# A two-block transformer kernel: expert selection issued in step with the weight splits, masks as full-row matmuls, and a rebuilt head

## The chip, the cores and the metric

The kernel runs on one core of one Trainium2 chip, in one launch. The metric is the device time of that core in microseconds (us), the median of three runs. One further execution was recorded by the hardware profiler, and every line of a view below comes from it.

## What is computed

256 tokens of width 1024 pass through two transformer blocks, everything in float32:

```
h = modulate(rms_norm(x), shift, scale)            # shift, scale, gate from silu(c) @ ada_w
z = h @ w_in + b_in                                # first block: q, k, v, gates, attention q, k, v
hm = mlstm_chunkwise(conv-silu(q, k), v, gates)    # 4 heads of 128
qa, ka = rope(aq, positions), rope(ak, positions)  # 8 heads of 64
ya = causal softmax attention(qa, ka, va)
x += g1 * ((sig(ga)*(ym @ p_mlstm) + sig(gb)*(ya @ p_moba)) @ w_out)
x += g2 * ((silu(h2 @ w_gate) * (h2 @ w_up)) @ w_down)
# second block
x += gate_m * (concat(pool_mixer, ssd_mixer) @ w_out_2)   # state-space mixer, 16 heads
q = h @ w_query; s1, s2 = q1 @ sub_keys1, q2 @ sub_keys2  # 8 heads, 128 keys each
v1, i1 = top_k(s1, 16); v2, i2 = top_k(s2, 16)
top_s, pos = top_k(v1[:, None] + v2[None, :], 16)         # 16 of 256 sums
out = sum over the chosen experts of softmax(top_s) * gelu(h . expert_down[i]) * expert_up[i]
x += gate_f * out; return rms_norm(x)
```

The kernel doesn't gather experts: it forms h . expert_down for all 16384 of them (128 slabs of 128x1024, the function `dblock`), multiplies by a sparse weight that the selection gives (`gstage`), and multiplies with all of expert_up.

## The kernel before

**Weights and matmuls.** Every weight slab is a 128x1024 float32 tile (512 KB) that comes by DMA on SyncE's queue. The slab is split into a high part `hi` (ScalarE, L213) and a low part `lo = raw - hi` (L218 on VectorE, or L216 on GpSimd), and every product is three fp32r matmuls, hi by high, hi by low, lo by high (`mm3`, L273). A block of 128 output rows takes 24 such matmuls of 256 columns. `prep` (L198) runs the list `items` two slabs ahead of the matmuls; `hi` and `lo` have three buffers each, raw slabs four and two more (`raw`, `ada`). `cur["gp"]` says that every gp-th split goes to GpSimd; 0 means none.

**Order.** The program is written in the order of the functions. A scheduler with a timing model of its own then fixes the order of instructions on each engine. `after(ins, prev)` (L89) is an edge without a semaphore that keeps `ins` behind `prev` on one engine. Background work is written as generators in `gens`; `tick()` (L295) emits one step of the first one, once per block or so.

**Head** (L128 to L455). The row c is loaded and spread over 128 partitions by two one-row matmuls (L380); the V bias row `bv` is loaded (4 KB, L138) and spread likewise (L423, L424). The squares of x are summed: four tiles of 128x512, squared on ScalarE (two) and GpSimd (two, L412), added on VectorE (L415), then summed over partitions by two matmuls (L316) in float32. `rstd` follows (Ln, Exp on ScalarE), then for each of eight k steps: two columns of the modulation (L230, VectorE), the modulated tile of x (L332 to L334), two slabs split, 36 matmuls of 256 columns (L452 to L454) and 6 of 512 (`mv`). At the end of the k steps `late1` (L393) loads constants, among them the positions (`posr`, spread by DMA) and the constants' tiles `cst0`, `cst1`.

**Rope angles** (L489 to L510). Behind the k steps the angles are reduced into plus or minus pi by nine VectorE instructions on 128x256, then Sin, Abs, Sin on ScalarE give `sin_t` and `cos_t`, which `rope` (L631) reads.

**Attention scores** (`moba`, L659). For the two halves of the tokens (tt = 1, then 0) and four groups c, one PSUM tile `ps` holds two heads: each a float32 matmul with 64 rows (L671; two instructions each) on partitions 0 to 63 or 64 to 127, and a mask added by a bf16 matmul of 128 rows and 128 columns (L672). VectorE takes row maxima (L674, L675), ScalarE the exponentials (L679), VectorE normalizes (L690), and TensorE transposes (L699 to L701). A score PSUM tile is one of five `sp` tiles.

**State-space masks** (L922 to L933). For 16 heads: a matmul of 48 rows and 384 columns (L929), two bf16 mask matmuls of 128 columns (L930, L931), two exponentials on ScalarE (L932, L933).

**Expert selection** (`topk`, L1083). Four generators, one per half of the heads and half of the tokens, 16 to 18 steps each: searches of eight maxima in 128 or 256 values (MAX8, FIND_INDEX8, MATCH_REPLACE8), the table of sums `cand`, one-hot comparisons `eq`, the softmax `gat`. A step is emitted after each of the query blocks 8 to 15 and of the first 64 slabs of expert_down; gp is 2 for the query blocks from 8 on and for slabs 0 to 27, then 0.

**Sparse weights** (`gstage`, L1194). 32 groups of eight tokens per half: one-hot tiles A and B on VectorE (L1198 to L1205), 16 small matmuls (L1210), a product into W (L1214). Half 0 runs beside slabs 64 to 127 of expert_down, half 1 beside expert_up.

## Time and profile before

| | us |
|---|---|
| median of three runs | 1427.33 (1427.19 to 1429.57) |
| the profiled execution | 1433.29 |
| its span, first to last instruction | 1431.5 |
| TensorE matmul busy | 1389.7 (97%) |
| VectorE busy | 1155.1 (81%) |
| ScalarE busy | 708.8 (50%) |
| GpSimd busy | 61.3 (4%) |

Matmuls overlap: one of 256 columns is shown as 0.28 us long, and the next one begins 0.12 us after it. So a busy TensorE may still lose time, and the number of matmuls that begin in a stretch says more than its busy share. The granted clock is 0.989 of full speed over the span, so it fell somewhere.

### The profile page before, as it was taken

Reading aid. Unit: us, or ns where it says so; the run is one execution under the profiler, and the core shown is the slowest. Engines: PE = TensorE matmul, PEld = TensorE weight load, DVE = VectorE, ACT = ScalarE, POOL = GpSimd, SP = SyncE. Lnnn points to the kernel's source line nnn. Section 1 sums busy time; section 2 is a strip of 40 time slices with the busy share of each in tenths; the row PEclk is TensorE's granted clock in tenths of the full one; section 3 lists DMA queues with packets and bytes.
Section 4 is the critical chain, followed back from the end, with each engine's and each line's share of the span. In section 5 each row is a group of like instructions: output and inputs, shape, how many; then the busy total and the mean of one; then the engine's idle time right before and its main releaser. Section 6 shows DMA issues by size and latency. Waiting matters only on the chain.

```text
span 1431.5 us, 28913 instructions
## 1 busy us (share of the span) xinstructions
PE 1389.7 (97%) x11842; PEld 1341.2 (94%) x11842; DVE 1155.1 (81%) x1995; ACT 708.8 (50%) x1052; POOL 61.3 (4%) x50
## 2 busy tenths in 40 slices
PE   8999989999999999998899999999999999999997
PEld 6888779899999788998899999999999999999997
DVE  7999558988888597789956978989689999675554
ACT  4555465554546846555554544444444443444443
POOL 0000000000000000123420000000000000000001
PEclk9999889999999999999999999999999999999999
DMA  9988416699995353554455555555655555676663
GB/s 319 341 289 314 148 47 192 229 350 343 330 317 207 104 155 125 163 161 149 162 188 181 177 166 174 163 165 172 180 164 161 177 161 172 200 215 213 208 205 103
DMA packets 78921, 285.92 MB, mean 200 GB/s; under 512 B 8786, under 2 KB 9186, under 8 KB 78660
## 3 DMA queue, kind: packets, MB, share of 16 engines
q1 hardware_dynamic: 78484, 282.60, 60.6%
q8 instruction: 93, 1.52, 0.4%
q0 software_dynamic: 304, 1.47, 0.3%
q14 instruction: 40, 0.33, 0.1%
HBM read 282.99 MB, written 1.05 MB: 198 GB/s over the span
## 4 chain that ended last, share of the span: by engine, by line
PE 85%; DVE 10%; ACT 2%; DMA 2%; issue 1%; SPq 0%; DVEq 0%; ACTq 0%
PE pp L274 17%; PE pp L276 17%; PE pp L275 17%; PE sp L1271 9%; PE sp L1274 8%; PE sp L1275 8%; DVE lo L218 3%; PE pp L1210 2%; ACT hi L213 1%; PE sp L671 1%; DMA raw<-in_wst 0%; DVE raw L230 0%; DMA ada<-in_wst 0%; DVE M L965 0%; PE sp L929 0%
## 5 line engine op out<-in xcount | busy, mean ns | idle before, releaser
L213 ACT ACTIVATE hi<-raw 128x1024 fp32r<-128x1024 f32 x382 | 404.6, 1060 | 562.7 <-PE pp L275 282.9
L218 DVE TENSOR_TENSOR lo<-raw,hi 128x1024 fp32r<-128x1024 f32 x364 | 450.3, 1238 | 141.3 <-ACT hi L213 140.5
L276 PE MATMUL pp<-nH,lo 128*128 128x256 f32 x1064 | 301.6, 285 | 16.1 <-DVE lo L218 16.1
L274 PE MATMUL pp<-nH,hi 128*128 128x256 f32 x1064 | 300.0, 283 | 1.5 <-ACT fs L107 0.9
L275 PE MATMUL pp<-nL,hi 128*128 128x256 f32 x1064 | 300.3, 283 | 0.0
L1271 PE MATMUL sp<-wHL,hi 128*128 128x256 f32 x992 | 279.5, 283 | 0.0
L1274 PE MATMUL sp<-wHL,hi 128*128 128x256 f32 x992 | 277.7, 281 | 0.0
L1275 PE MATMUL sp<-wHL,lo 128*128 128x256 f32 x992 | 273.8, 281 | 0.0
L274 PE MATMUL pp<-hH,hi 128*128 128x256 f32 (+1 forms) x824 | 237.0, 288 | 1.3 <-ACT sg L721 1.3
L276 PE MATMUL pp<-hH,lo 128*128 128x256 f32 (+1 forms) x824 | 234.6, 285 | 0.0
L275 PE MATMUL pp<-hL,hi 128*128 128x256 f32 (+1 forms) x824 | 233.6, 284 | 0.0
L276 PEld LDWEIGHTS pp<-nH,lo 128*128 128x128 f32 x1064 | 200.2, 189 | 19.4 <-DVE lo L218 19.3
L274 PEld LDWEIGHTS pp<-nH,hi 128*128 128x128 f32 x1064 | 200.7, 189 | 2.1 <-ACT fs L107 1.1
L275 PEld LDWEIGHTS pp<-nL,hi 128*128 128x128 f32 x1064 | 200.5, 189 | 0.1
L1271 PEld LDWEIGHTS sp<-wHL,hi 128*128 128x128 f32 x992 | 188.2, 190 | 0.0
L1274 PEld LDWEIGHTS sp<-wHL,hi 128*128 128x128 f32 x992 | 188.0, 189 | 0.0
L1275 PEld LDWEIGHTS sp<-wHL,lo 128*128 128x128 f32 x992 | 185.9, 190 | 0.0
L274 PEld LDWEIGHTS pp<-hH,hi 128*128 128x128 f32 x824 | 157.1, 191 | 2.7 <-ACT sg L721 1.5
L276 PEld LDWEIGHTS pp<-hH,lo 128*128 128x128 f32 x824 | 157.2, 191 | 1.1 <-issue 0.7
L275 PEld LDWEIGHTS pp<-hL,hi 128*128 128x128 f32 x824 | 157.3, 191 | 0.7 <-issue 0.5
L1214 DVE SCALAR_TENSOR_TENSOR W<-pp,W 128x512 f32<-128x512 f32 x64 | 86.1, 1346 | 22.3 <-PE pp L1210 22.3
L213 ACT ACTIVATE hi<-ada 128x1024 fp32r<-128x1024 f32 x52 | 55.1, 1059 | 67.3 <-PE pp L275 37.9
(442 smaller groups left out, 2146.9 us busy)
## 6 DMA issues: line engine op xcount, KB each, us to landing
raw<-in_edn SPq DMA_DIRECT2D x128, 512.0 KB, 3.6
raw<-in_eup SPq DMA_DIRECT2D x128, 512.0 KB, 4.2
raw<-in_ada SPq DMA_DIRECT2D x64, 512.0 KB, 5.0
raw<-in_win SPq DMA_DIRECT2D x34, 512.0 KB, 4.4
ada<-in_ada SPq DMA_DIRECT2D x32, 512.0 KB, 5.1
raw<-in_wgu SPq DMA_DIRECT2D x32, 512.0 KB, 4.5
ada<-in_win SPq DMA_DIRECT2D x18, 512.0 KB, 4.5
raw<-in_wdn SPq DMA_DIRECT2D x15, 512.0 KB, 5.8
```

The costliest lines, as they stand in the source:

```text
L213: S.activation(hi, raw, AF.Copy)
L218: cur["lo"] = V.tensor_tensor(lo, raw, hi.bitcast(F32), OP.subtract)
L274: m = PE.matmul(ps, lh, rh, start=start, stop=False)
L275: PE.matmul(ps, lh, rl, start=False, stop=False)
L276: PE.matmul(ps, ll, rh, start=False, stop=stop)
L671: PE.matmul(ps[:, j * T:j * T + ns], ro[rows, r, tt * P:(tt + 1) * P], ro[rows, 4 + r, :ns], start=True, stop=False)
L1210: PE.matmul(ps[:, t * 64:(t + 1) * 64], A[:, t].rearrange("p n d -> p (n d)"), B[:, j, t].rearrange("p n d -> p (n d)"), start=(j == 0), s ...
L1214: V.scalar_tensor_tensor(wv, ps.rearrange("p (t n) -> p t n", t=GT), 1.0 / GSC, wv, OP.mult, OP.mult)
L1271: m = PE.matmul(o, hi[:, b], wH, start=first, stop=False, skip_group_check=True)
L1274: PE.matmul(o, hi[:, b], wL, start=False, stop=False, skip_group_check=True)
L1275: return PE.matmul(o, lo[:, b], wH, start=False, stop=last, skip_group_check=True)
```

## The change

Six edits. (1) The bias row `bv` comes by a DMA that spreads it over 128 partitions (512 KB, in `late1`), in place of a 4 KB load and two matmuls. (2) Squares 1 and 3 of x move from GpSimd to VectorE, and the two halves are added before a single summing matmul. (3) The rope angles are computed in the head; `posr` and a small tile `inv` (inverse frequencies and pi/2) are loaded from GpSimd's queue. (4) Scores: two groups share a step, their 64-row matmuls alternate between the two halves of the partitions, and one fp32r mask matmul of 256 columns serves both heads of a PSUM tile. (5) State-space masks: the operand is padded with zeros to 128 rows, and the two mask matmuls become one of 256 columns in fp32r; the mask operands are made on ScalarE. (6) Expert selection: edges put the steps of `topk` and the first instruction of each `gstage` group behind the newest `lo` on VectorE; gp becomes 4, from query block 8 to slab 55.

```diff
+    posr = q1.tile([P, T], I32, name="posr")
+    G.dma_start(posr, bass.AP(tensor=I["pos"].tensor, offset=I["pos"].offset, ap=[[0, P], [1, T]]))
+    inv = const.tile([P, 2], F32, name="inv")
+    G.dma_start(inv, I["inv"])
-    dma(brow[0:1], I["bv"])
...
+    def paced(ins):
+        after(ins, cur["lo"])
+        return ins
...
         def late1():
             dma(cst[0], I["cst0"])
-            dma(posr, bass.AP(tensor=pa.tensor, offset=pa.offset, ap=[[0, P], [1, T]]))
+            load_bias_row(bv, I["bv"])
             dma(wif, I["wif"])
             dma(cst[1], I["cst1"])
...
+        trig = q1.tile([P, 4, T], F32, name="trig", tag="qk")
+        ang = trig[:, 0]
+        V.tensor_copy(ang, posr)
+        V.tensor_scalar(ang, ang, inv[:, 0:1], None, op0=OP.mult)
...
         sx = q1.tile([P, 512], F32, name="sx", tag="rt")
...
-                    G.tensor_tensor(sq, src, src, OP.mult)
+                    V.tensor_tensor(sq, src, src, OP.mult)
...
-        for k in range(2):
-            sumsq_mm(nps[:, :T], sx[:, k * T:(k + 1) * T], k, 2)
+        V.tensor_tensor(sx[:, :T], sx[:, :T], sx[:, T:], OP.add)
+        sumsq_mm(nps[:, :T], sx[:, :T], 0, 1)
-        for j in range(2):
-            bps = sp()
-            PE.matmul(bps, ones[0:1], brow[0:1, j * 512:(j + 1) * 512], start=True, stop=True)
-            S.activation(bv[:, j * 512:(j + 1) * 512], bps, AF.Copy)
...
-                    ps = sp()
-                    rows = slice(64 * (c % 2), 64 * (c % 2) + 64)
-                    for j in range(2):
-                        r = 2 * (c // 2) + j
-                        PE.matmul(ps[:, j * T:j * T + ns], ro[rows, r, tt * P:(tt + 1) * P], ro[rows, 4 + r, :ns], start=True, stop=False)
-                        PE.matmul(ps[:, j * T + tt * P:j * T + ns], identb, trib, start=False, stop=True)
+                    if c % 2 == 0:
+                        pair = [sp(), sp()]
+                        for j in range(2):
+                            r = 2 * (c // 2) + j
+                            for i, ps in enumerate(pair):
+                                rows = slice(64 * i, 64 * i + 64)
+                                PE.matmul(ps[:, j * T:j * T + ns], ro[rows, r, tt * P:(tt + 1) * P], ro[rows, 4 + r, :ns],
+                                          start=j == 0, stop=False, skip_group_check=True)
+                        for ps in pair:
+                            PE.matmul(ps.rearrange("p (g s) -> p g s", g=2)[:, :, tt * P:ns], identr,
+                                      trir[:, None, :].to_broadcast([P, 2, P]), start=False, stop=True, skip_group_check=True)
+                    ps = pair[c % 2]
...
-        ArS = q3.tile([48, 384], F32R, name="ArS")
+        ArS = q3.tile([P, 384], F32R, name="ArS")
+        G.memset(ArS.bitcast(F32), 0.0)
...
-                PE.matmul(ab[:, :P], identb, trib, start=False, stop=False, skip_group_check=True)
-                PE.matmul(ab[:, T:384], identb, trib, start=False, stop=True, skip_group_check=True)
+                PE.matmul(ab.rearrange("p (g s) -> p g s", g=2)[:, :, :P], identr, trir[:, None, :].to_broadcast([P, 2, P]),
+                          start=False, stop=True, skip_group_check=True)
...
-                    V.max(v[:, h, 0:8], s_[:, h])
+                    paced(V.max(v[:, h, 0:8], s_[:, h]))
...
-                cur["gp"] = 2
+                cur["gp"] = 4
...
-            cur["gp"] = 2 if n2 < 28 else 0
+            cur["gp"] = 4 if n2 < 56 else 0
...
-            V.tensor_tensor(A, iob.rearrange("p (n d) -> p n d", d=2)[:, None].to_broadcast([P, GT, 64, 2]),
+            paced(V.tensor_tensor(A, iob.rearrange("p (n d) -> p n d", d=2)[:, None].to_broadcast([P, GT, 64, 2]),
```

## Rows read from the trace of the kernel before

**Rows 1.** Busy time by stretch: us, then busy (instructions) per engine, clock, DMA, GB/s
```profile
16.00:60.00 44.00, 43.24 (x297) 39.41 (x297) 41.41 (x75) 18.90 (x24) 0.00 (x0) 1.00 0.97 339
...
167.00:184.00 17.00, 17.00 (x65) 13.15 (x65) 6.86 (x24) 8.71 (x30) 0.00 (x0) 0.50 0.10 32
...
473.40:493.70 20.30, 20.30 (x139) 15.42 (x138) 11.30 (x20) 17.43 (x44) 0.00 (x0) 1.00 0.39 118
...
608.00:728.00 120.00, 107.64 (x889) 105.62 (x888) 114.88 (x360) 62.27 (x92) 44.36 (x17) 1.00 0.48 155
728.00:775.00 47.00, 47.00 (x399) 47.00 (x398) 18.39 (x15) 21.30 (x32) 2.40 (x1) 1.00 0.64 202
...
1040.00:1215.00 175.00, 175.00 (x1838) 173.63 (x1838) 170.80 (x229) 71.91 (x69) 0.00 (x0) 1.00 0.53 165
```

**Rows 2.** Waits, 608 to 728 us: total us, times, longest
```profile
PE pp L276 <- DVE lo L218: 11.9, 8, 2.4
```

**Rows 3.** Timeline in expert selection, GpSimd and VectorE: start, duration, instruction
```profile
678.37 2.39 POOL L216 TENSOR_TENSOR lo<-raw,hi 128x1024 fp32r<-128x1024 f32 x1 [2.64 <-ACT hi L213]
...
678.58 3.26 DVE L218 TENSOR_TENSOR lo<-raw,hi 128x1024 fp32r<-128x1024 f32 x1
```

**Rows 4.** VectorE by line, 608 to 728 us: busy us, mean ns, idle before
```profile
L218 DVE TENSOR_TENSOR lo<-raw,hi 128x1024 fp32r<-128x1024 f32 x21 | 31.9, 1522 | 4.8 <-ACT hi L213 4.8
...
L1097 DVE MAX8 v<-s 128x8 f32<-128x128 f32 x24 | 5.1, 273 | 2.8 <-ACT s L1093 2.8
```

**Rows 5.** Timeline of TensorE through the attention scores
```profile
161.76 0.70 PE L671 MATMUL sp<-ro 64*128 64x256 f32 x2
162.39 0.23 PE L672 MATMUL sp<-trib,identb 128*128 128x128 bf16 x1
162.55 0.70 PE L671 MATMUL sp<-ro 64*128 64x256 f32 x2
...
176.76 0.79 PE L671 MATMUL sp<-ro 64*128 64x128 f32 x2
...
177.71 0.79 PE L671 MATMUL sp<-ro 64*128 64x128 f32 x2
...
186.05 0.28 PE L699 MATMUL sp<-cst,P 128*128 128x128 f32 x1
```

**Rows 6.** Timeline of TensorE: three column tiles of 32, six instructions
```profile
134.45 0.65 PE L585 MATMUL sp<-E,ones 128*32 128x256 f32 x6
134.91 0.41 PE L586 MATMUL sp<-E,ones 128*32 128x128 f32 x6
```

**Rows 7.** Waits, 161.7 to 190 us
```profile
ACT P L107 <- DVE nm L675: 7.1, 3, 4.8
```

**Rows 8.** Timeline of TensorE in the state-space masks, two heads
```profile
473.47 0.44 PE L929 MATMUL sp<-ArS,id 48*128 48x384 f32 x1
...
474.06 0.44 PE L929 MATMUL sp<-ArS,id 48*128 48x384 f32 x1
```

**Rows 9.** Waits, 38 to 120 us
```profile
PE pp L274 <- ACT sg L721: 1.3, 1, 1.3
```

**Rows 10.** The rope angles' tile: four of the nine, ns min/median/max, first and last start
```profile
L505 DVE SCALAR_TENSOR_TENSOR trig<-trig x4: 417/418/426, 61.3 to 64.9; 128x256 f32<-128x256 f32 x4
```

**Rows 11.** Timeline of the head, TensorE and ScalarE
```profile
12.28 3.78 PE L423 MATMUL sp<-vm,ones 1*128 1x512 f32 x4
...
14.16 0.49 ACT L333 ACTIVATE hH<-mt,mod 128x256 fp32r<-128x256 f32 x1
...
15.98 1.22 PE L452 MATMUL sp<-hH,hi 128*128 128x256 f32 x4
```

**Rows 12.** Timeline in the sparse weights, VectorE and TensorE
```profile
1108.83 0.77 DVE L1205 TENSOR_TENSOR B<-B,gd 128x512 f16<-128x512 f16 x2
1109.50 1.23 DVE L218 TENSOR_TENSOR lo<-raw,hi 128x1024 fp32r<-128x1024 f32 x1
...
1110.72 0.64 PE L1210 MATMUL pp<-B,A 128*128 128x64 f16 x16
```

More of the change, by code (lines that the diff above doesn't have):

```diff
@@ L43 @@
 NPRM = _o
-CST = [("ident", 128), ("iota", 128), ("invf", 1), ("half_pi", 1)]
+CST = [("ident", 128), ("iota", 128)]
 CS1 = [("mA", 256), ("tri", 128), ("selr", 512), ("sel4", 512), ("selt", 128), ("rotT", 128)]
@@ L388, in two_block_kernel @@
         cst[1] = q1.tile([P, NCST[1]], F32, name="cst1")
-        posr = q1.tile([P, T], I32, name="posr")
         bv = q1.tile([P, D], F32, name="bv")
@@ L403, in two_block_kernel @@
         cos_t = q1.tile([P, T], F32, name="cos_t")
+        trig = q1.tile([P, 4, T], F32, name="trig", tag="qk")
+        ang = trig[:, 0]
+        V.tensor_copy(ang, posr)
+        V.tensor_scalar(ang, ang, inv[:, 0:1], None, op0=OP.mult)
+        kk = trig[:, 1]
+        V.tensor_scalar(kk, ang, 1.0 / TWO_PI, MAGIC, op0=OP.mult, op1=OP.add)
+        k2 = trig[:, 2]
+        V.tensor_scalar(k2, kk, MAGIC, None, op0=OP.subtract)
+        rest = TWO_PI
+        parts = []
+        for bits in (5, 13, 21):
+            c = np.floor(rest * 2.0 ** bits) / 2.0 ** bits
+            parts.append(float(c))
+            rest -= c
+        parts.append(float(rest))
+        for c in parts:
+            V.scalar_tensor_tensor(ang, k2, -c, ang, OP.mult, OP.add)
+        V.tensor_scalar(ang, ang, PI_F, -PI_F, op0=OP.min, op1=OP.max)
+        act(sin_t, ang, AF.Sin)
+        aab = trig[:, 3]
+        S.activation(aab, ang, AF.Abs)
+        act(cos_t, aab, AF.Sin, scale=-1.0, bias=inv[:, 1:2])
         sx = q1.tile([P, 512], F32, name="sx", tag="rt")
@@ L488, in two_block_kernel @@
         silu_set()
-        trig = q1.tile([P, 4, T], F32, name="trig", tag="ro")
-        ang = trig[:, 0]
-        V.tensor_copy(ang, posr)
-        V.tensor_scalar(ang, ang, cs_("invf"), None, op0=OP.mult)
-        kk = trig[:, 1]
-        V.tensor_scalar(kk, ang, 1.0 / TWO_PI, MAGIC, op0=OP.mult, op1=OP.add)
-        k2 = trig[:, 2]
-        V.tensor_scalar(k2, kk, MAGIC, None, op0=OP.subtract)
-        rest = TWO_PI
-        parts = []
-        for bits in (5, 13, 21):
-            c = np.floor(rest * 2.0 ** bits) / 2.0 ** bits
-            parts.append(float(c))
-            rest -= c
-        parts.append(float(rest))
-        for c in parts:
-            V.scalar_tensor_tensor(ang, k2, -c, ang, OP.mult, OP.add)
-        V.tensor_scalar(ang, ang, PI_F, -PI_F, op0=OP.min, op1=OP.max)
-        act(sin_t, ang, AF.Sin)
-        aab = trig[:, 3]
-        S.activation(aab, ang, AF.Abs)
-        act(cos_t, aab, AF.Sin, scale=-1.0, bias=cs_("half_pi"))
         zp = [q1.tile([P, 3 + T], F32, name="zp%d" % i) for i in range(4)]
@@ L653, in two_block_kernel @@
         yaH, yaL = ya[:, 0], ya[:, 1]
-        identb = q1.tile([P, P], BF, name="identb")
-        V.tensor_copy(identb, ident)
-        trib = q1.tile([P, P], BF, name="trib")
-        V.tensor_copy(trib, cs_("tri"))
+        identr = q1.tile([P, P], F32R, name="identr")
+        S.activation(identr, ident, AF.Copy)
+        trir = q1.tile([P, P], F32R, name="trir")
+        S.activation(trir, cs_("tri"), AF.Copy)
         def moba():
@@ L881, in two_block_kernel @@
         cbT = q3.tile([P, 2, 384], F32, name="cbT")
[L882 to L883 removed]
+        ArS = q3.tile([P, 384], F32R, name="ArS")
+        id16 = q3.tile([P, 16], F32R, name="id16")
+        G.memset(ArS.bitcast(F32), 0.0)
+        G.memset(id16.bitcast(F32), 0.0)
         S.activation(id16[0:32], ident[0:32, 0:16], AF.Copy)
         S.activation(id16[32:48], ident[0:16, 0:16], AF.Copy)
[L886 to L889 removed]
+        identr = q3.tile([P, P], F32R, name="identr")
+        S.activation(identr, ident, AF.Copy)
+        trir = q3.tile([P, P], F32R, name="trir")
+        S.activation(trir, cs_("mB"), AF.Copy)
         yv = q3.tile([P, 8, T], F32, name="yv")
@@ L1387, in _layout @@
     half = np.arange(32, dtype=f) / f(32)
-    cput("invf", np.tile(f(10000.0) ** (-half), 4)[:, None].astype(f))
-    cput("half_pi", np.full((P, 1), np.pi / 2, f))
     cput("invc", np.broadcast_to(np.concatenate([1.0 / np.minimum(np.arange(16) + 1, w) for w in (2, 4, 8, 16)]).astype(f), (P, 64)))
@@ L1441, in _layout @@
         "prm": prm, "cst0": cst[0], "cst1": cst[1], "cst2": cst[2], "pos": C(a["positions"]),
+        "inv": C(np.stack([np.tile(f(10000.0) ** (-half), 4), np.full(P, np.pi / 2)], 1).astype(f)),
         "bv": C(np.concatenate([b_in[o_mv:o_mv + M], b_in[o_av:o_av + M]])[None]),
```

33 lines of the change are left out of this document (13 added, 20 removed).

## The prediction

> **What bounds the kernel now.** I read the page first (busy shares, then the chain that ended last, nearly all of it matmul lines), then the busy time by stretch, then the waits stage by stage, and the timeline only where a stretch fell short. TensorE is the bound: from 728 to 775 us, where nothing disturbs it, 399 matmuls begin in 47 us, 0.1178 us each, and a block of 24 takes 2.83 us [rows 1]. What a change can win is the time in which fewer begin. The reader is to see four such places. In expert selection, 608 to 728 us, only 889 matmuls begin in 120 us, where 0.1178 us each would allow 1019 [rows 1]; the waits name one cause, eight stalls for `lo`, 11.9 us together [rows 2]. In the attention scores the granted clock is 0.50, the lower of its two levels (1.2 against 2.4 GHz), for 17 us from 167 us on, in which only 65 matmuls begin [rows 1]; before it fell, TensorE alternated between 64-row scores and bf16 masks [rows 5]. In the state-space masks each head takes 0.59 us of TensorE [rows 8]. In the head the first weight matmul begins at 15.98 us [rows 11]. From there to 60 us the DMA engines are 97% busy [rows 1].
>
> **The change part by part.** The sum is made against the profiled execution, 1433.29 us, which stands 5.96 us above the median of the runs.
>
> *Expert selection.* The stalls arise because VectorE's order is fixed in advance and selection steps stand ahead of a `lo` that TensorE soon needs; VectorE is busy 114.88 of the 120 us there and only 18.39 of the following 47 [rows 1]. The edges hold each step behind the newest `lo`, which belongs to a slab two blocks ahead, and spread the steps over 72 blocks (8 query blocks and 64 slabs), one each. Does VectorE have the time? Of the 114.88 us, 31.9 are 21 splits [rows 4]; the other 83.0 are three of the four selections (24 first searches, eight per selection, [rows 4]), 27.7 us each, 110.6 for four. GpSimd takes every fourth split of 8 + 56 blocks, 16 in place of 18, so VectorE keeps 56 at the mean of 1.52 us [rows 4], 85.1 us. Together 195.7 us, against 72 x 2.83 = 203.8 us of matmuls. It fits with 8 us to spare, and unevenness is covered by two blocks of lead. I take the whole 11.9 us, as -12; the ends are 0 (each stall comes back) and the shortfall in matmuls, (1019 - 889) x 0.1178 = -15.3. What is late next: a step of `topk` itself, which only the sparse weights wait for, dozens of blocks later. If the lead were eaten up, a stall would cost its 1.5 us as now.
>
> Against this part: while GpSimd subtracts for 2.39 us from 678.37, VectorE's own subtraction is held from 678.58 to 681.84 [rows 3]; 16 such holds at the present rate are inside the mean of 1.52 us. By the Trainium skill (GPSIMD Engine Reference, section 1, Specifications), GpSimd shares its SBUF interfaces with VectorE, and VectorE's instructions with two SBUF inputs contend. By that rule, where the later slabs get GpSimd splits for the first time, each may cost VectorE all of its duration; the rival below prices that from the rows.
>
> *Attention scores.* Now one head costs 0.79 us of TensorE with 256 columns (0.63 until the mask, 0.16 for it) and 0.95 with 128 at the lower clock [rows 5], 8 x 0.79 + 8 x 0.95 = 13.9 us of the 24.3 between 161.76 and the first transpose at 186.05. Afterwards two heads on different halves of the rows may run at the same time. No row shows that for row tiles; the nearest shows it for column tiles: six float32 instructions of 256 columns in three column tiles take 0.46 us in all [rows 6], so a round of two takes 0.46 at most. A pair of groups then costs two rounds, two masks of 0.12 and one change of shape, about 0.63 - 0.46 = 0.2: 1.4 us, and 0.9 with half the columns, for four pairs 4.6 us, 9.3 less. If row tiles don't overlap, it is four rounds, 2.3 us per pair, about 7.4 in all and 6.5 less. The weight matmuls at the lower clock, about 8 of the 17 us, would cost half at the higher one, 4 less. TensorE alone would thus give up to -13.3. But the transposes need the exponentials, and ScalarE is served by VectorE's row maxima: it waited 7.1 us for them in this stage [rows 7]. That wait is what can vanish; its own work can't. I take -7; the ends are -13.3 and -2.
>
> The Trainium skill (TensorEngine Tiling, Performance Considerations, PSUM Bottleneck) says that tiling speeds up TensorE but not the emptying of PSUM, which may then be the limit. By that rule the -7 holds; by TensorE's rows alone the sum would be 6.3 us lower.
>
> *State-space masks.* Per head 0.59 us [rows 8]. A 384-column matmul and a 256-column one in one shape cost (1.5 + 1) x 0.1178 = 0.29. Over 16 heads that is -4.7 for TensorE. But ScalarE is busy 17.43 of the 20.3 us [rows 1], and the exponentials are its work: only 2.9 us can go. Two more copies for the mask operands cost it some 0.5. I take -2; ends -4.7 and 0. The zeroing on GpSimd lies long before its use.
>
> *Rope angles.* Nine VectorE instructions of at most 0.42 us [rows 10], under 3.8 us, leave the stretch after the k steps, and the two mask copies with them. TensorE waits little for VectorE behind them: the one wait worth naming is 1.3 us, for a ScalarE copy queued behind late slabs [rows 9]. I take -1.3; ends -2.7 and 0.
>
> *Head.* The two bias matmuls hold TensorE from 12.28 to 15.98, while the first modulated tile is ready at 14.65 [rows 11]: up to 1.3 us. Against that, VectorE now has the angles (3.8), two squares and a fold in front of the first tile, and waits for `posr` from GpSimd's queue, behind which the squares, the Silu-to-Ln table change and rstd would queue. The bias tile is 512 KB in front of `wif` and the next slabs on SyncE's queue, 1.5 us at 339 GB/s [rows 1], less the 128 KB of `posr` that go away there. I take 0; ends -1.3 and +3.
>
> Sum: -12 - 7 - 2 - 1.3 + 0 = -22.3, so 1411.0 us profiled and 1405.0 for the median, if the same stalls stand in the unprofiled runs.
>
> **The rivals.** *VectorE is full in expert selection.* GpSimd's splits move to slabs 28 to 55, seven of them; at 2.39 us of VectorE each [rows 3] that is 16.7 us where 8 are to spare, so 9 us of stalls return: the part gives -3, the time is 1414. For it: 96% use by my sum. Against it: the mean of 1.52 us already holds such stalls, and the number of GpSimd splits falls.
>
> *The clock falls again in the scores.* 64-row work and waits remain there. Then the weight matmuls keep the lower rate (4 us back), the part gives -3, and the time is 1409.
>
> *The edges change nothing.* They are only edges of order; if the stalls come from `hi` or GpSimd's `lo` coming late, not from the searches, the 12 us stay: 1417. Against it: all eight name VectorE's `lo` [rows 2].
>
> *The sparse weights stall (slower).* The edge on A also holds in `gstage`, where VectorE is busy 170.80 of 175 us [rows 1]. Today a group's last B is done at 1109.60 and its matmuls begin at 1110.72 [rows 12], 1.1 us to spare. If the edge puts A behind two more splits (2 x 1.23 [rows 12]), the group is 1.4 us late, and TensorE, which works in order, stops. 32 groups would cost 45 us: 1450. It decides from 22.3 / 64 = 0.35 us per group. Against it: no such wait exists today, splits and A alternate already, and the step was emitted behind the same split.
>
> **How the numbers follow.** A measurement of this kernel can tell about 0.2%, 2.9 us, from no change. Chances: the forecast 0.50, VectorE full 0.18, the clock 0.15, edges without effect 0.09, sparse weights stalling 0.08. All but the last are faster, less 0.05 for their worst ends meeting: faster 0.87, same 0.05, slower 0.08. The range runs from 1394, three quarters of the way to the best ends (-37 in all), to 1420, past the third rival; it leaves out the last one and the far ends.
>
> **What would show it.** Right: in the stretch of the slabs no wait of L276 for `lo`, one selection step between two splits on VectorE, about 1010 matmuls in 120 us; a clock of 1.00 from 160 to 200 us and transposes some 7 us earlier against their neighbours; ScalarE above 90% in the masks; no change before 60 us. Wrong: waits of L1210 for A or B, waits for `lo` beside GpSimd's splits, a clock of 0.50 in the scores, or a first weight matmul well after 16 us.

## The result, and the profile after

The changed kernel takes **1411.45 us** (median of 4 runs, 1410.35 to 1415.28) against 1428.45 for the kernel before (4 runs, 1427.19 to 1433.03). The ratio is 0.988, with a 95% interval of 0.985 to 0.991, so 17.0 us are won where the prediction said 22.3 (it had 1405.0 for the median). A second measurement of the same kernel on another chip gave 0.9888 (0.9867 to 0.991). The profiled execution took 1411.06 us (span 1409.2).

Busy time by stretch in the kernel after; the columns are those of [rows 1], and the third line is the masks' stretch, moved with them:

```profile
16.00:60.00 44.00, 35.96 (x250) 34.25 (x251) 37.70 (x67) 19.19 (x26) 0.00 (x0) 1.00 0.84 297
167.00:184.00 17.00, 14.77 (x103) 12.45 (x102) 12.47 (x38) 14.36 (x44) 0.00 (x0) 0.96 0.33 94
466.60:486.90 20.30, 20.30 (x166) 20.30 (x166) 12.70 (x21) 20.04 (x51) 0.00 (x0) 1.00 0.46 147
608.00:728.00 120.00, 120.00 (x1013) 120.00 (x1012) 103.72 (x318) 64.70 (x95) 24.23 (x10) 1.00 0.61 181
```

Three of the four places where matmuls were missing are filled: 1013 begin in 120 us of expert selection (889 before), 103 in 17 us of scores with the clock at 0.96 (65 at 0.50), 166 in the masks' 20.3 us (139), with ScalarE now busy 20.04 of them. The head went the other way: 250 in place of 297, and DMA at 297 GB/s in place of 339.

Summed by stages, the profiles before and after show what each part brought; the second profile is that of the repeat, the first experiment below. Each stage runs from the start of one TensorE instruction to that of the next: the last product of `hi` with `hL` in the k steps (L475, the last matmul but one), the first score (L672), the last product with V (L715), the first small matmul of the state-space mixer (L922), the third residual sum (L371), the first sparse-weight matmul (L1217), the first and the last one with expert_up (L1278). The lines of the profile after, start and duration first:

```profile
24.04 1.43 PE L474 MATMUL sp<-hH,hi 128*128 128x256 f32 x5 [10.47 <-ACT hH L339]
71.56 0.28 PE L475 MATMUL pp<-hL,hi 128*128 128x256 f32 x1
165.90 1.13 PE L672 MATMUL sp<-ro 64*128 64x256 f32 x8
202.16 0.40 PE L715 MATMUL sp<-PT,va 128*64 128x128 f32 x4
457.87 0.61 PE L922 MATMUL sp<-cst,dt 16*128 16x16 f32 x4
576.55 0.60 PE L371 MATMUL sp<-acc,ones 128*128 128x256 f32 x2
815.93 0.64 PE L1217 MATMUL pp<-B,A 128*128 128x64 f16 x16
1015.27 0.28 PE L1278 MATMUL sp<-wA,hi 128*128 128x256 f32 x1
1397.69 0.28 PE L1278 MATMUL sp<-wHL,hi 128*128 128x256 f32 x1
```

| stage, us | before | after | after, second profile | forecast of the change |
|---|---|---|---|---|
| H: head and k steps | 65.19 | 71.56 (+6.4) | 72.29 (+7.1) | 0 |
| R: to the first score | 96.57 | 94.34 (-2.2) | 94.08 (-2.5) | -1.3 |
| S: scores to the last product with V | 44.09 | 36.26 (-7.8) | 36.18 (-7.9) | -7 |
| T: to the state-space mixer | 258.75 | 255.71 (-3.0) | 259.54 (+0.8) | none |
| M: mixer with its masks, to the third residual sum | 123.24 | 118.68 (-4.6) | 117.18 (-6.1) | -2 |
| X: expert selection, to the first sparse weights | 252.65 | 239.38 (-13.3) | 239.38 (-13.3) | -12 |
| G: first half of the sparse weights | 197.07 | 199.34 (+2.3) | 199.36 (+2.3) | 0 (a rival) |
| U: with expert_up | 382.53 | 382.42 | 382.46 | 0 |
| sum | 1420.09 | 1397.69 (-22.4) | 1400.47 (-19.6) | -22.3 |

The sum of the first profile meets the forecast to 0.1 us, but by chance: a loss of 8.7 us in H and G that was not forecast is covered by R, S, T, M and X together, and 3.0 us of that lie in T, for which nothing was forecast.

**The head after.** ScalarE's timeline (start, duration, instruction):

```profile
18.62 0.42 ACT L107 ACTIVATE sin_t<-trig 128x256 f32<-128x256 f32 x1 [3.86 <-DVE trig L425]
20.20 0.49 ACT L107 ACTIVATE cos_t<-trig,inv 128x256 f32<-128x256 f32 x1
20.71 1.28 ACT L94 ACT_TABLE_LOAD   x1
22.00 0.47 ACT L107 ACTIVATE lnt<-sp,eps 128x256 f32<-128x256 f32 x1
22.51 0.42 ACT L107 ACTIVATE rstd<-lnt 128x256 f32<-128x256 f32 x1
23.48 0.91 ACT L339 ACTIVATE hH<-mt,mod 128x256 fp32r<-128x256 f32 x2 [0.55 <-DVE mt L338]
```

and VectorE's, the first and the last of the nine angle instructions with one split between:

```profile
6.21 0.29 DVE L410 CAST trig<-posr 128x256 f32<-128x256 int32 x1 [4.88 <-DMA posr<-in_pos]
16.02 1.22 DVE L220 TENSOR_TENSOR lo<-raw,hi 128x1024 fp32r<-128x1024 f32 x1
18.30 0.28 DVE L425 TENSOR_SCALAR trig<-trig 128x256 f32<-128x256 f32 x1
```

Both Sin run from the Silu table (no load stands between Silu and them) and were written ahead of the load of the Ln/Exp table, so Ln, Exp and the first modulated tile stand behind them. They wait for VectorE's chain of angles, and that chain takes from 6.21 to 18.58: its 3.2 us of instructions alternate with squares, modulation columns and splits, the last two of 1.22 us each. TensorE's summing matmuls begin long before (12.35), and the first weight matmul comes at 24.04 in place of 15.98 [rows 11]. The table load itself is the small part: Cos ends at 20.69, Ln begins at 22.00, 1.31 us for the switch. The Trainium skill (ScalarE: Activation LUTs, What ACT_TABLE_LOAD costs) puts a switch at about 2.66 us, load and drain together. The trace doesn't agree: it shows half of that, and the measured figure decides.

The k steps regain little of the 8 us because TensorE has little to spare there. Their 336 matmuls take 49.3 us before, from the first to the last, and 47.6 us after. At the pace at which they follow each other here, 0.118 us for each of the 288 with 256 columns and 0.23 for each of the 48 with 512, they need 45 us (an estimate). So some 4 us could be regained and 1.7 were. The two stretches, before and after (columns of [rows 1]):

```profile
15.98:65.31 49.33, 48.57 (x336) 44.52 (x336) 46.63 (x86) 22.34 (x32) 0.00 (x0) 1.00 0.98 347
```

```profile
24.04:71.68 47.64, 47.64 (x335) 45.32 (x336) 38.69 (x67) 20.60 (x29) 0.00 (x0) 1.00 0.86 317
```

Before, the DMA engines were full (0.98). After, TensorE is busy throughout and DMA is not full (0.86, 317 GB/s), and while TensorE stood, from 16 to 24 us, DMA had moved 335 GB/s. So it is TensorE's own work that holds the k steps now, and they end 6.4 us later.

### The profile page after: what moved, and what is told of

It is laid out like the page before. It is cut to its first block, busy times and chain, and to the rows that moved or that the text cites. A ratio compares the mean times of both kernels' runs of the same rounds, so it can differ in the third digit from the quotient of the medians.

```text
span 1409.2 us, 28867 instructions
## 1 busy us (share of the span) xinstructions
PE 1365.5 (97%) x11812; PEld 1331.5 (94%) x11812; DVE 1157.1 (82%) x1996; ACT 708.7 (50%) x1054; POOL 52.5 (4%) x50
## 4 chain that ended last, share of the span: by engine, by line
PE 93%; DVE 3%; ACT 2%; issue 1%; DMA 0%; DVEq 0%; SPq 0%; ACTq 0%
PE pp L276 19%; PE pp L278 19%; PE pp L277 19%; PE sp L1278 9%; PE sp L1282 9%; PE sp L1281 9%; PE pp L1217 2%; DVE lo L220 1%; PE sp L474 1%; ACT hi L215 1%; PE sp L475 1%; PE sp L476 1%; PE sp L1099 1%; DMA xT<-in_xT 0%; DVE raw L232 0%
## 5 line engine op out<-in xcount | busy, mean ns | idle before, releaser
L1278 PE MATMUL sp<-wHL,hi 128*128 128x256 f32 x992 | 279.7, 283 | 0.0
L1282 PE MATMUL sp<-wHL,lo 128*128 128x256 f32 x992 | 276.7, 281 | 0.0
L1278 PEld LDWEIGHTS sp<-wHL,hi 128*128 128x128 f32 x992 | 188.2, 190 | 0.0
L1221 DVE SCALAR_TENSOR_TENSOR W<-pp,W 128x512 f32<-128x512 f32 x64 | 86.2, 1347 | 22.3 <-PE pp L1217 22.3
```

The costliest lines, as they stand in the source:

```text
L1221: V.scalar_tensor_tensor(wv, ps.rearrange("p (t n) -> p t n", t=GT), 1.0 / GSC, wv, OP.mult, OP.mult)
L1278: m = PE.matmul(o, hi[:, b], wH, start=first, stop=False, skip_group_check=True)
L1282: return PE.matmul(o, lo[:, b], wH, start=False, stop=last, skip_group_check=True)
```

## The experiments

Each is an edit of the changed kernel. "Ratio" is to the kernel before on the same chip, with its 95% interval.

### The changed kernel again

> The changed kernel unaltered, to tell what one profile of it is worth. Three kernels with an earlier head reached the scores 2.2 to 5.3 us earlier than the changed kernel and gave this back between the first small matmuls of the state-space mixer and the third residual sum, where the changed kernel took 118.7 us and they took 120.1 to 123.0. Theory (the order of VectorE and ScalarE there, which the scheduler lays anew for each program, makes the difference): the repeat takes 118 to 119.5 us there again, and every other stretch within 0.5 us of its first profile. Rival (it differs from run to run, as the clock does): 120 us or more in the repeat.

Median 1413.71 us, ratio 0.9888 (0.9867 to 0.991). M took 117.18 us, below the expected 118; but T took 259.54 in place of 255.71, so "every other stretch within 0.5 us" was wrong. Two stretches, first of the first profile, then of the second:

```profile
250.00:300.00 50.00, 47.55 (x390) 46.62 (x390) 47.66 (x88) 28.07 (x44) 0.00 (x0) 1.00 0.81 290
540.00:560.00 20.00, 17.95 (x132) 17.24 (x131) 14.17 (x28) 10.52 (x21) 0.00 (x0) 0.91 0.48 146
```

```profile
250.00:300.00 50.00, 46.77 (x372) 45.85 (x371) 45.32 (x86) 28.17 (x44) 0.00 (x0) 0.97 0.76 263
540.00:560.00 20.00, 17.94 (x141) 17.12 (x141) 15.68 (x31) 12.09 (x23) 0.00 (x0) 1.00 0.50 157
```

With the same instructions in the same order on every engine, the granted clock falls in one execution where it doesn't in the other, and fewer matmuls begin there. The waits before are the same: from 205 to 208 us TensorE waits three times for 0.4 to 0.6 us in both, and from 208 to 212 us the clock is 1.00 in the first profile and 0.61 in the second. So from one profile T is known to some 4 us and M to 1.5; S, X, G and U repeat within 0.1 us.

### The head, step by step

Three kernels undo more and more of it. First only the place where the angles are written:

```diff
-        trig = q1.tile([P, 4, T], F32, name="trig", tag="qk")
...
-        act(cos_t, aab, AF.Sin, scale=-1.0, bias=inv[:, 1:2])
         sx = q1.tile([P, 512], F32, name="sx", tag="rt")
...
         silu_set()
+        trig = q1.tile([P, 4, T], F32, name="trig", tag="ro")
...
+        act(cos_t, aab, AF.Sin, scale=-1.0, bias=inv[:, 1:2])
         zp = [q1.tile([P, 3 + T], F32, name="zp%d" % i) for i in range(4)]
```

> The changed kernel with the angles written behind the k steps again; `posr` and `inv` still come early, so VectorE's nine angle instructions stay in the gaps of the head and only ScalarE's two Sin move behind the Silu table load after the k steps. Theory (ScalarE's order: Ln, Exp and the first modulated tile stand behind both Sin, and these wait for VectorE's chain): the first weight matmul comes at 17 to 19 us in place of 24.04, the k steps end at about 67 in place of 71.7, and the whole takes 1405 to 1408 us against 1411.5 for the changed kernel (ratio to the kernel before about 0.985). Rival (VectorE has too much in front of the first tile: squares, fold and nine angle instructions): the first weight matmul stays at 22 us or later and the time at 1410 to 1412.

The head did as the theory said. The timeline of this kernel:

```profile
17.23 0.51 ACT L339 ACTIVATE hH<-mt,mod 128x256 fp32r<-128x256 f32 x1 [2.41 <-DVE mt L338]
17.79 1.43 PE L452 MATMUL sp<-hH,hi 128*128 128x256 f32 x5 [4.73 <-ACT hH L339]
20.46 0.42 ACT L509 ACTIVATE trig<-trig 128x256 f32<-128x256 f32 x1 [1.77 <-DVE trig L506]
```

VectorE still has its angles in the gaps, seven of the nine ahead of the first modulated tile (Abs, which follows the ninth, runs at 20.46), and yet the first weight matmul comes at 17.79: the order on ScalarE was the cause, not VectorE's load. The k steps end at 66.0. But the whole took 1415.61 us (1413.27 to 1417.84), ratio 0.9903 (0.9869 to 0.9936), and neither theory had that: R is 97.66 us (94.34 in the changed kernel) and M 122.87 (118.68).

Next also `posr` behind the k steps:

```diff
-    posr = q1.tile([P, T], I32, name="posr")
-    G.dma_start(posr, bass.AP(tensor=I["pos"].tensor, offset=I["pos"].offset, ap=[[0, P], [1, T]]))
...
             dma(cst[0], I["cst0"])
+            dma(posr, bass.AP(tensor=I["pos"].tensor, offset=I["pos"].offset, ap=[[0, P], [1, T]]))
             load_bias_row(bv, I["bv"])
```

> The changed kernel with the angles behind the k steps and `posr` loaded there too, as in the kernel before; the bias row's DMA, the squares on VectorE and the fold stay. Theory (the squares and the fold cost the 2 us by which the summing matmul is later, 12.35 against 10.27, and nothing else): first weight matmul at 17 to 18 us, end of the k steps at 66 to 67, then the angles cost about 2 us again before the scores: 1407 to 1409 us. Rival (the bias row's DMA of 512 KB delays the slabs behind it): the first weight matmul is early, but the k steps and the gate matmuls behind them stay 3 us or more late against the kernel before.

First weight matmul at 15.88, k steps done at 63.61, 1.6 us before the kernel before: squares on VectorE, the fold and the bias DMA cost the head nothing, and the rival of a delayed slab queue falls. Total 1410.71 us (1403.96 to 1411.24), ratio 0.9849 (0.9808 to 0.989); R is 97.96, M 120.07.

Then the whole head of before (the 4 KB load of the bias row and the moved angles are left out here):

```diff
...
-            load_bias_row(bv, I["bv"])
+            dma(posr, bass.AP(tensor=I["pos"].tensor, offset=I["pos"].offset, ap=[[0, P], [1, T]]))
...
-                    V.tensor_tensor(sq, src, src, OP.mult)
+                    G.tensor_tensor(sq, src, src, OP.mult)
...
-        V.tensor_tensor(sx[:, :T], sx[:, :T], sx[:, T:], OP.add)
-        sumsq_mm(nps[:, :T], sx[:, :T], 0, 1)
+        for k in range(2):
+            sumsq_mm(nps[:, :T], sx[:, k * T:(k + 1) * T], k, 2)
...
+            PE.matmul(bps, ones[0:1], brow[0:1, j * 512:(j + 1) * 512], start=True, stop=True)
+            S.activation(bv[:, j * 512:(j + 1) * 512], bps, AF.Copy)
```

> The changed kernel with the whole head of the kernel before (bias row by matmul, squares on GpSimd, two summing matmuls, angles and `posr` behind the k steps); scores, masks and expert selection as changed. Theory (the head alone was mis-sized): first weight matmul at 16.0 us, k steps end at 65.3, scores begin at 161.8, total 4 us less than the changed kernel, about 1407 us. If the squares and the DMA bias row gain something by themselves, this run is slower than the one with only the angles moved back; by the first theory it is the same or up to 1.5 us faster. Rival (the late head was made up behind, so nothing is left of it at the scores): 1411 us.

First weight matmul at 15.37, k steps done at 64.61, scores at 160.62, as the theory had it; but 1410.21 us (1407.29 to 1415.19), ratio 0.9861 (0.9819 to 0.9903), as the rival had it. The edits to the head and the angles together thus neither won nor lost anything that these runs can tell. R is 96.01, M 123.03.

So a head 5.6 to 8 us shorter is for the greater part paid back in R and M (5.0 to 7.5 us there). All four kernels here with the angles behind the k steps (these three and the last one below) take 96.0 to 100.0 us in R and 120.1 to 123.0 in M; the eight profiles with the angles in the head and the new masks take 94.1 to 95.6 and 117.2 to 118.7. Part of this is the clock: it is 0.50 for 6.8 to 10.2 us of M in the four and for 3.4 to 6.8 us in the eight. With half of that time taken off, the four are at 116.7 to 117.9 us and the eight at 115.0 to 115.5, so 1 to 3 us are left. In R the forecast term, angles out of the stretch, is the likely reason; but with the same half taken off, the kernel with the whole old head has 94.3 us there, as much as with the angles in the head, so it isn't shown. M is 300 us later and its code the same in all. TensorE's waits from 440 to 592 us that differ, in the changed kernel, then in the one with only the angles moved:

```profile
PE pp L276 <- ACT mixP L1038: 1.3, 1, 1.3
PE pp L277 <- DVE mixP L1039: 0.7, 1, 0.7
```

```profile
PE pp L276 <- ACT mixP L1038: 1.9, 1, 1.9
PE pp L276 <- DVE mt L361: 1.3, 1, 1.3
PE pp L277 <- DVE mixP L1039: 1.1, 1, 1.1
```

The three waits of the second are 4.3 us, 2.3 more than the two of the first (the others are the same but for one of 0.3 us), and the clock fell once more there: 0.86 from 455 to 467 us, which is 1.7 us of the 12. Together that makes about the 4.2 us by which M is longer. VectorE's and ScalarE's instructions stand in another order there: the scheduler lays the whole program anew for each edit. That its order causes the waits is the likely reading; no run set that order by hand, so it is not shown.

### Expert selection

Without edges, with GpSimd's old share:

```diff
     def paced(ins):
-        after(ins, cur["lo"])
         return ins
...
-                cur["gp"] = 4
+                cur["gp"] = 2
...
-            cur["gp"] = 4 if n2 < 56 else 0
+            cur["gp"] = 2 if n2 < 28 else 0
```

> The changed kernel without the edges of order in expert selection and in the sparse weights, and with every second split on GpSimd up to slab 27 again; all else as changed. Theory (the selection steps ahead of `lo` were the stalls): waits of TensorE for VectorE's `lo` between 590 and 720 us come back, some 12 us in all; the stretch from the third residual sum to the first sparse weight matmul takes about 252 us in place of 238.8, the first half of the sparse weights about 2 us less, and the whole 1421 to 1424 us. Rival (the edges are only order and the gain came from a better start of the stretch): the stretch stays within 3 us of 238.8, total 1410 to 1414 us.

The theory holds: 1421.67 us (1420.83 to 1423.78), ratio 0.9944 (0.9926 to 0.9962); X takes 253.91 us, G 197.06, and the waits are like those of [rows 2]:

```profile
PE pp L278 <- DVE lo L220: 11.6, 8, 2.4
```

The edges with the old share (only the two lines with `gp`), and the new share without edges (only the line of `paced`):

> The changed kernel with GpSimd's share as before (every second split up to slab 27, none after), all edges kept. Theory (the edges alone take the stalls away, GpSimd's share is of no account): from the third residual sum to the first sparse-weight matmul 238 to 241 us as in the changed kernel (239.4). Rival (VectorE needs the relief of slabs 28 to 55, seven splits of 1.2 to 1.5 us): waits for `lo` come back in the second half of the slabs, 5 to 9 us, the stretch takes 244 to 249 us.

> The changed kernel without any of the edges, but with GpSimd's new share (every fourth split up to slab 55). Theory (the order is the cause): the waits for VectorE's `lo` stay, 8 to 12 us, and the stretch takes 249 to 254 us (253.9 without edges and with the old share). Rival (GpSimd's share is what helped): 239 to 244 us.

Edges alone: X 238.41 us, no wait for `lo`, 1411.13 us, ratio 0.987 (0.9847 to 0.9893). Share alone: X 252.56 us, 8.0 us of waits for `lo` (4.7 for VectorE's, 3.3 for GpSimd's), 1419.65 us, ratio 0.9935 (0.9915 to 0.9955). Both theories hold: the edges are worth 13.2 to 15.5 us in X, GpSimd's share 1.4 us without them and 1.0 the other way with them. Without edges the new share has 3.6 us less of waits, but the clock is 0.50 for longer in that profile (6.8 us of X in place of 3.4). VectorE's subtractions from 608 to 728 us (busy us, mean ns) show a second thing, in the changed kernel, with edges and old share, and with neither:

```profile
L220 DVE TENSOR_TENSOR lo<-raw,hi 128x1024 fp32r<-128x1024 f32 x31 | 37.8, 1220 | 11.2 <-ACT hi L215 11.0
```

```profile
L220 DVE TENSOR_TENSOR lo<-raw,hi 128x1024 fp32r<-128x1024 f32 x24 | 29.7, 1239 | 14.1 <-ACT hi L215 13.9
```

```profile
L220 DVE TENSOR_TENSOR lo<-raw,hi 128x1024 fp32r<-128x1024 f32 x19 | 30.0, 1580 | 7.3 <-ACT hi L215 7.3
```

The mean was 1522 ns before [rows 4], raised by holds beside GpSimd [rows 3]. With the edges the holds are all but gone (one of 0.4 us is left with the old share), although GpSimd makes 18 splits in this stretch in the second kernel as in the third: VectorE searches while GpSimd subtracts, and its own subtraction comes after. One such turn of the changed kernel:

```profile
658.13 2.40 POOL L218 TENSOR_TENSOR lo<-raw,hi 128x1024 fp32r<-128x1024 f32 x1 [9.23 <-ACT hi L215]
```

```profile
658.61 0.29 DVE L1108 FIND_INDEX8 x<-v,s 128x8 uint32<-128x128 f32 x1
660.88 1.23 DVE L220 TENSOR_TENSOR lo<-raw,hi 128x1024 fp32r<-128x1024 f32 x1 [1.98 <-ACT hi L215]
```

The search beside GpSimd keeps its 0.29 us; the subtraction begins when GpSimd has ended (660.53). The prediction weighed the rule of the Trainium skill (GPSIMD Engine Reference, section 1, Specifications) that VectorE's instructions with two SBUF inputs contend with GpSimd. The traces agree: without edges five of the 19 subtractions begin well inside a split on GpSimd and take 2.24 to 3.25 us, and in the changed kernel none of the 31 meets one. Three others begin just ahead of a split on GpSimd: they keep their 1.20 us, and it is GpSimd's that takes 3.1 to 3.9 us in place of 2.4.

### The edge in the sparse weights

```diff
-            paced(V.tensor_tensor(A, iob.rearrange("p (n d) -> p n d", d=2)[:, None].to_broadcast([P, GT, 64, 2]),
-                                  i1d[:, tsl, None, :].to_broadcast([P, GT, 64, 2]), OP.is_equal))
+            V.tensor_tensor(A, iob.rearrange("p (n d) -> p n d", d=2)[:, None].to_broadcast([P, GT, 64, 2]),
+                            i1d[:, tsl, None, :].to_broadcast([P, GT, 64, 2]), OP.is_equal)
```

> The changed kernel without the edge on A in the sparse weights; the edges in the four selections stay. Theory (the edge there is the slower rival in small: A waits for a split it does not need): the stretch from the first sparse-weight matmul to the first matmul with expert_up falls from 199.3 to 197.1 us, no wait for A is left, and the whole takes 2.2 us less than the changed kernel in the same batch. Rival (the three waits for A have another cause, as the order of the last selection steps): the stretch stays at 199 us.

G is 197.04 us and no wait for A is left, where the changed kernel has

```profile
PE pp L1217 <- DVE A L1205: 1.8, 3, 0.6
```

1408.23 us (1406.74 to 1409.51), ratio 0.9853 (0.983 to 0.9875), against 1413.71 for the changed kernel on the same chip. Of these 5.5 us the edge explains 2.3; most of the rest lies in T (259.54 against 256.09), which the edit does not touch, and where the clock is 0.50 for 6.8 us in the one profile and never in the other.

### The scores

```diff
-                        for ps in pair:
-                            PE.matmul(ps.rearrange("p (g s) -> p g s", g=2)[:, :, tt * P:ns], identr,
-                                      trir[:, None, :].to_broadcast([P, 2, P]), start=False, stop=True, skip_group_check=True)
+                        for j in range(2):
+                            for ps in pair:
+                                PE.matmul(ps[:, j * T + tt * P:j * T + ns], identb, trib, start=False, stop=j == 1, skip_group_check=True)
```

> The changed kernel with its paired scores, but with the bf16 masks of 128 columns of the kernel before, one per head. Theory (running two heads on the two halves of the rows is the gain, and it keeps the clock up because TensorE is done with the scores in half the time): the stretch from the last norm sum to the first transpose takes 15.1 to 17 us (15.1 changed, 25.2 before), the clock stays at 1.00 up to 180 us, total within 2 us of the changed kernel. Rival (the mix of float32 scores and bf16 masks lets the clock fall): a clock near 0.50 between 168 and 180 us, the stretch takes 19 us or more, total 3 to 5 us longer.

S is 36.17 us, the stretch from the last norm sum to the first transpose 14.7 (15.1 in the changed kernel), the clock 1.00 from 167 to 184 us, the time 1414.12 us, ratio 0.9874 (0.9856 to 0.9892). The full-row masks win nothing here; the pairing is the gain. Pairing is two things at once, matmuls that alternate between the halves and one step where there were two, and no run separates them. But the overlap itself is seen: eight instructions of a pair in 1.06 us, where two took 0.63 until the mask [rows 5]. The first pair in the changed kernel, and with bf16 masks:

```profile
165.90 1.13 PE L672 MATMUL sp<-ro 64*128 64x256 f32 x8
166.96 0.51 PE L675 MATMUL sp<-trir,identr 128*128 128x256 f32 x2
167.39 1.13 PE L672 MATMUL sp<-ro 64*128 64x256 f32 x8
```

```profile
166.66 1.13 PE L672 MATMUL sp<-ro 64*128 64x256 f32 x8
167.73 0.40 PE L676 MATMUL sp<-trib,identb 128*128 128x128 bf16 x4
168.05 1.14 PE L672 MATMUL sp<-ro 64*128 64x256 f32 x8
```

Four heads take 1.49 us (1.39 with bf16 masks), where one took 0.79 [rows 5].

### The state-space masks

```diff
-                se = id16[:, h:h + 1].to_broadcast([P, P])
+                se = id16[:, h:h + 1].to_broadcast([48, P])
...
-                PE.matmul(ab.rearrange("p (g s) -> p g s", g=2)[:, :, :P], identr, trir[:, None, :].to_broadcast([P, 2, P]),
-                          start=False, stop=True, skip_group_check=True)
+                PE.matmul(ab[:, :P], identb, trib, start=False, stop=False, skip_group_check=True)
+                PE.matmul(ab[:, T:384], identb, trib, start=False, stop=True, skip_group_check=True)
```

(with `ArS`, `id16` and the mask tiles of before)

> The changed kernel with the state-space masks of the kernel before (48 rows, two bf16 masks of 128 columns). Theory (one mask matmul in one shape gives TensorE back some time, and ScalarE's exponentials bound the rest): from the first to the last mask matmul 17 to 18 us (14.1 changed, 17.5 before), from the first small matmul of the mixer to the third residual sum 121 to 123 us in place of 118.7, total 2 to 4 us longer than the changed kernel. Rival (the transposes and products behind wait for ScalarE and VectorE anyway): the longer stretch stays at 118 to 119.5 us and the total does not move.

From the first to the last mask 19.0 us (14.1 changed), M 124.88, 1417.30 us (1413.2 to 1419.05), ratio 0.9895 (0.9876 to 0.9913). The theory holds in its direction; the sizes are above it because the clock fell in this profile (0.87 from 467 to 480 us, 1.00 in the changed kernel). The kernel before, with its clock at 1.00 there, took 17.5, so the masks are worth 3.4 us up to the last of them. In M as a whole they are worth 4.5: it is 6.2 us longer, and 1.7 of that is the clock (0.50 for 10.2 us of M in place of 6.8). That is all by which M had become shorter. And M is longer here, with the angles in the head, than the 123.24 of the kernel before, which has them behind the k steps; so it isn't their place as such that makes M short or long. By the medians the masks are worth 3.6 to 5.9 us against the two measurements of the changed kernel, by the ratios 1 to 2; their intervals overlap.

### Two kernels that mend both losses

Both leave out the edge on A. In one the angles are written behind `rstd`, with their own table loads:

```diff
         act(nA, pc("alog")[0:16], AF.Exp)
+        trig = q1.tile([P, 4, T], F32, name="trig", tag="qk")
...
+        silu_set()
+        act(sin_t, ang, AF.Sin)
...
+        act(cos_t, aab, AF.Sin, scale=-1.0, bias=inv[:, 1:2])
+        lnexp()
         accs = [sp() for _ in range(5)] + [pp()]
```

> The changed kernel without the edge on A, and with the angles written behind rstd: Ln and Exp come first on ScalarE, then a table load, the two Sin, and a load back, all beside the k steps. Theory (only the Sin ahead of Ln hurt the head): first weight matmul at 17.5 to 18.5 us, k steps end at 66 to 67, from the gate columns to the first mLSTM score 27.3 us as in the changed kernel, attention scores at 160 to 162 us, sparse weights 197 us; total 1404 to 1409 us, the lower end if the 4 to 5 us won at the head last to the end. Rival (they are given back in the state-space mixer, as in the three kernels with an earlier head): 1408 to 1410 us. Second rival (two more table loads and the Sin delay the k steps): first weight matmul above 20 us.

**1406.14 us** (1403.74 to 1406.23), ratio 0.982 (0.9804 to 0.9837), clear of the changed kernel's interval in either measurement. It beats both kernels. Its ScalarE in the head:

```profile
14.70 0.41 ACT L107 ACTIVATE rstd<-lnt 128x256 f32<-128x256 f32 x1
15.12 1.28 ACT L94 ACT_TABLE_LOAD   x1
17.46 0.51 ACT L339 ACTIVATE hH<-mt,mod 128x256 fp32r<-128x256 f32 x1 [1.05 <-DVE mt L338]
18.82 0.40 ACT L107 ACTIVATE sin_t<-trig 128x256 f32<-128x256 f32 x1
```

The first weight matmul comes at 18.02, the k steps end at 65.26, DMA is back at 337 GB/s from 16 to 60 us, scores begin at 160.85, and M stays at 118.38. Of the 6.3 us won in H, R (95.59) and S (37.10) give back 2.1, and M none. One expected number failed: from the gate columns to the first mLSTM score 30.9 us, not 27.3. What the mended head alone is worth is not clear of the noise: without the edge on A alone the ratio was 0.9853 (0.983 to 0.9875), and the intervals touch.

The other has the angles and `posr` behind the k steps (the edits of the second head kernel):

> The changed kernel without the edge on A, and with the angles and `posr` behind the k steps as before; the bias row's DMA, the squares on VectorE and the fold stay. Theory (both losses of the changed kernel are mended and add up): first weight matmul at 15.9 us, attention scores at 161.6 us, sparse weights 197 us, total 1404 to 1408 us. Rival (what the head wins is given back by the order in the state-space mixer): 1408 to 1410 us, as without the edge on A alone.

1405.94 us (1403.21 to 1409.75), ratio 0.9818 (0.98 to 0.9836). The first weight matmul is at 16.64, but the scores begin at 163.72 (R 99.99, with the clock at 0.50 for 6.8 us of it) and M is 121.78. Its profiled execution, 1409.75, is the longest of its five, so its profile speaks for the rival and its median for the theory; this stays open.

## Why the prediction was right, and where it was wrong

**Direction and mechanism: right.** Faster, inside the range, in expert selection and in the scores by the reasons given. That the whole came so near is partly luck: losses that were not forecast and gains above the forecast cancelled.

*Expert selection* (-12 forecast, -13.3 measured, twice). The step held with its reason: the searches ahead of `lo` were the stalls, as taking the edges away and keeping them alone show. The rival of a full VectorE fell: VectorE is busy 103.72 of 120 us. The forecast's bound counted on the mean of 1.52 us per split; the edges brought it to 1.22, which was not foreseen.

*Attention scores* (-7 forecast, -7.8). Row tiles overlap: 1.49 us per pair where 1.4 was estimated. From the first score to the first transpose 10.1 us were won (24.3 to 14.2), and 2.3 given back before the last product, in the place where the prediction held the term short of -13.3: ScalarE. But its queue is held by more than exponentials. Its timeline in the kernel after:

```profile
179.26 1.28 ACT L94 ACT_TABLE_LOAD   x1
180.55 1.06 ACT L107 ACTIVATE smo<-smo 128x1024 f32<-128x1024 f32 x1
182.81 0.86 ACT L707 ACTIVATE PT<-sp 128x384 f32<-128x384 f32 x2
183.56 3.63 ACT L107 ACTIVATE sg<-sg 128x4096 f32<-128x4096 f32 x1
187.19 1.28 ACT L94 ACT_TABLE_LOAD   x1
189.21 0.85 ACT L707 ACTIVATE PT<-sp 128x384 f32<-128x384 f32 x2
```

A table load and the activation of `smo` stand ahead of the first copies of the transposes, and TensorE waits 2.2 us for these (PT). Then a gate function over 4096 columns and a second load stand between the copies; ScalarE is busy 9.97 of the 10 us from 180 on, and the granted clock falls to 0.63 there. The rival of the clock was thus half right: it stays at 1.00 through the scores, as forecast, and falls after them. The fall costs little, since TensorE is held there anyway: from 183 to 194 us the clock is 0.55 here and 0.84 in the kernel without the edge on A, and 37 matmuls begin in both.

*State-space masks* (-2 forecast, M -4.6 and -6.1): the reason for the cut from -4.7 to -2 did not hold. The text lowered TensorE's gain to what ScalarE could follow. ScalarE is indeed full there, all of the 15.84 us from its first exponential to its last (17.88 before, 15.19 of them busy), which is 2.0 us less. But no wait of TensorE for an exponential is listed. From the first head's matmul to the last mask it takes 14.25 us in place of 17.96, and it keeps these 3.7 us to the end of M. The two mask copies, 0.29 and 0.31 us, lie at 438 and 441 us, before M. The run with the old masks gives 4.5 us for the masks, so the term was short by about 2.5; the further 1.5 us of the second profile are the clock (0.50 for 3.4 us of M in place of 6.8).

*Rope angles* (-1.3 forecast, R -2.2 and -2.5): right in sign, about 1 us short, if the angles are the reason (see the kernel with the old head).

*Head* (0 forecast, ends -1.3 and +3; +6.4 and +7.1 measured): **the step that failed.** The text named what would be held ("behind which the squares, the Silu-to-Ln table change and rstd would queue"), but put it down to VectorE's load and the landing of `posr`, priced it by the angles' own 3.8 us and did not see the two Sin in ScalarE's queue. The squares were not held (TensorE sums them from 12.35 on). What counts is when the last of the nine ends on a queue that alternates with splits, 18.58 us, since ScalarE waits there with Ln behind it; with only the Sin moved away the first weight matmul came at 17.79 in place of 24.04. "No change before 60 us" fell with it; "a first weight matmul well after 16 us", named as a sign that the text is wrong, came.

*Sparse weights* (0 forecast; the slower rival +45 at the worst): +2.3. The rival had place and sign, a wait of L1217 for A, but three groups of 32 pay 0.6 us each, not every group 1.4.

**The size.** By the profiles the sum was met, -22.4 and -19.6 against -22.3; by the medians -17.0 came. Part of the profiles' difference belongs to no edit: T, in which of the edits only the two mask copies lie, ranges from 255.6 to 262.0 us over the fourteen profiles. Most of that is the clock: with half of the time at 0.50 taken off, T is 254.4 to 257.0 in all of them. The profiled execution of the kernel before, 1433.29 us, lies above its medians in all four measurements (1428.45 to 1431.56), while those of the changed kernel lie at theirs. Without T the first profile gives 6.4 - 2.2 - 7.8 - 4.6 - 13.3 + 2.3 = -19.2; the 2 us from there to the measured -17.0 stay open, since the kernel before was profiled once. So the forecast missed 8.7 us of loss in the head and the sparse weights, and the four terms that came out larger than forecast (R 0.9, S 0.8, M 2.6 and X 1.3 us) paid 5.6 of it back.

## What to carry to other kernels

Price an instruction moved into a busy head by when the last of its chain can end on the queues it passes, not by its duration, and ask which activation-table group it is put ahead of. An edge of order that keeps background steps behind the newest urgent instruction can be worth more than any rebalancing between engines, but put it only where a wait shows it is needed. And when a scheduler lays the order of the whole program anew, an edit must be judged by its stage as well as by the total, with a second profile of the same kernel to know what a stage is worth.

## What the runs showed of the hardware that was not expected

- One program in one order differs by 2.8 us between two profiles on two chips. The granted clock falls behind the same short waits in one and not in the other (390 and 372 matmuls from 250 to 300 us).
- VectorE's subtractions cost 1.24 us with the edges and 1.58 without, both with 18 splits on GpSimd in the same 120 us: it matters when they run. Of two subtractions that meet, the one that began first keeps its time and the other is held (2.24 to 3.25 us on VectorE, 3.1 to 3.9 on GpSimd). Searches beside a split on GpSimd keep their time (FIND_INDEX8 0.29 us).
- Half-row matmuls on the two halves of the array: eight instructions of 64 rows and 256 columns in 1.06 us; a bf16 mask behind them is no dearer (0.32 us for four of 128 columns) than an fp32r one (0.43 for two of 256).
